# Every third weight block's remainder from a negated copy on ScalarE and an adding DMA, in place of a VectorE subtraction

## The chip, the cores and the metric

The kernel runs on one NeuronCore of a Trainium2 chip: TensorE for the products, VectorE and ScalarE for elementwise work, GpSimd, and SyncE (SP), which issues most transfers. The metric is the device time of one execution in microseconds (us); smaller is better. In the profile TensorE is PE (its weight loads are PEld), VectorE is DVE, ScalarE is ACT, GpSimd is POOL, and a q behind an engine's name is its queue.

## The reference

Two layers over 256 tokens of width 2048, all in float32: attention with a residual, then a feed-forward with a residual, and at the end a last norm. Every dense product takes a weight matrix from HBM that is used once.

```python
def rms_norm(x, g):
    y = x * lax.rsqrt(jnp.mean(x * x, axis=-1, keepdims=True) + EPS)
    return y * g

def sq_relu_mlp(h, w1, w2):          # w1 2048 x 8192, w2 8192 x 2048
    return jnp.square(jax.nn.relu(h @ w1)) @ w2

def reference(x, ...):
    for i in range(2):
        hn = rms_norm(x, mixer_norms[i])
        if i == 0:
            x = x + neighbourhood_attention(hn, na_wqkv, na_rpb, na_wo)
        else:
            x = x + dilated_attention(hn, dil_wqkv, dil_wo)
        g, w1, w2 = ffns[i]
        x = x + sq_relu_mlp(rms_norm(x, g), w1, w2)
    return rms_norm(x, final_norm)
```

The first attention has 16 heads with a learned bias over a 64-wide grid; the second has three groups of 8 heads with different dilations, and a softmax over all three together.

## The kernel before

**Weight blocks.** All weights are cut into 400 blocks of 4 x 128 rows and 512 columns (1 MB). One block is one step of the program. In order: 48 blocks for q, k and v of the first attention (four groups of 8 for q and k and 4 for v), 16 for its output, 128 for the first feed-forward (four times 16 of w1 and 16 of w2), 72 and 8 for the second attention, 128 for the second feed-forward.

**Precision by two parts.** TensorE's fast float32 form (F32R) keeps fewer bits, so each operand is cut into a rounded part (`hi`; for weights the tile wh) and the remainder (`lo`; tile wl), and the product of the two remainders is dropped. `split` (line 103) makes both: ScalarE copies the source into the rounded form (line 104), VectorE subtracts that from the source (line 105). `prep(i, u)` (line 86) does so for half u of block i, a tile of 128 x 1024; a block's first half is the first two of its four 128-row pieces.

**Two forms of product.** `gemm_cols` (lines 134 and 136): the weights stand still and the activations stream, two products for each piece and column tile. These are the q and k blocks and w1, in column groups of four blocks k = 0 to 3. Block k = 0 takes its quarters as two column tiles with the first half, the same with the second half, then the other two column tiles, so the second half is wanted after one quarter; the others go piece by piece. `gemm_rows` (lines 155 to 157): the activations stand still, three products; these are v, the output projections and w2, piece by piece.

**Order.** The order on each engine is the order in which the loop at the end of `tile_encoder` issues the work (line 736 on). In step i, after the second quarter, the first half of block i + 2 is prepared (line 746), after the step its second half (line 759), then the load of block i + 5 is issued on SP (line 760). Work that belongs to a step goes between: `evac` copies finished sums out of PSUM (the copies at line 144 on ScalarE, the additions at 146 and 271 on VectorE), `post` and the tasks do norms, softmax (Exp at line 407), the square of the feed-forward (line 474) and the cutting of the activations hT, on the same two engines.

**Buffers.** `wpool` holds three whole blocks, so the load of block i + 5 goes where block i + 2 lay and waits until both its halves have been read. `hlpool` holds four halves of wh and four of wl, that is two blocks: the half of block i + 2 goes where that half of block i lay, and its preparation waits until TensorE has read that for the last time.

Of the kernel before, what the change touches and what calls it, by code (L numbers as in the profile page):

```python
# [8 lines left out]
F32 = mybir.dt.float32  # L9
F32R = mybir.dt.float32r  # L10
AF = mybir.ActivationFunctionType
ALU = mybir.AluOpType
AX = mybir.AxisListType

P = 128
# [11 lines left out]


class Step:
    """One weight block [4 x 128, 512], the products that it takes part in (in four  # L30
    quarters) and the work that goes with them: tasks have a part on the tensor engine
    after a quarter, evac reads the finished sums, post follows."""

    def __init__(self, src, quarters):
        self.src = src
# [7 lines left out]
def tile_encoder(ctx: ExitStack, tc: tile.TileContext, ins, out):  # L43
    nc = tc.nc
# [13 lines left out]
    x = const.tile([P, 2, D], F32, name="x")  # L58
# [9 lines left out]

    x_in = ins["x"].rearrange("(t p) d -> p t d", p=P)

# [1 line left out]
    steps = []  # L72

    def load(i):
# [11 lines left out]
    def prep(i, u):  # L86
        if i >= len(steps):
            return
        s = steps[i]
        hi = hlpool.tile([P, 2, 512], F32R, name="wh", tag="wh")  # L90
        lo = hlpool.tile([P, 2, 512], F32R, name="wl", tag="wl")
        part = s.w[:, 2 * u:2 * u + 2, :]
        if i:
            split(hi, lo, part)
        else:
            for a in range(2):
                split(hi[:, a], lo[:, a], part[:, a])
        s.hi[u], s.lo[u] = hi, lo
# [6 lines left out]
        nc.vector.tensor_tensor(out=dst_lo, in0=src, in1=dst_hi.bitcast(F32), op=ALU.subtract)  # L105

    def three(o, left, right, start, stop):
        """o += left.T @ right, both in two parts; the product of the two rests is below float32."""
        nc.tensor.matmul(o, left[0], right[0], start=start, stop=False)  # L109
        nc.tensor.matmul(o, left[0], right[1], start=False, stop=False)  # L110
        nc.tensor.matmul(o, left[1], right[0], start=False, stop=stop)  # L111

# [1 line left out]
    def gemm_cols(w, col, xT, nk, done):  # L114
        acc = {}
        made = []
# [39 lines left out]
        nc.tensor.matmul(o, xh, wl, start=False, stop=False)  # L156
        nc.tensor.matmul(o, xl, wh, start=False, stop=stop)  # L157

# [1 line left out]
    def gemm_rows(w, col, xT, ks, acc, first_k, last_k, apart=False):  # L160
        made = []
        for k in ks:
# [10 lines left out]
            made.append(s)  # L173
        return made

# [1 line left out]
    class Norm:  # L177
        def __init__(self, n, perm):
            self.n, self.perm = n, perm
# [68 lines left out]
            nc.vector.tensor_copy(self.r, self.r_ps[:, 0, 0:4].rearrange("p (t u) -> p t u", u=2)[:, :, 0])  # L248

    def rsqrt_mean(ss):  # L250
        """1 / sqrt(mean + eps) of the sums of squares: a root, its reciprocal and one step of Newton's on it."""
        a = small.tile([P, 2], F32, name="ms", tag="ms", bufs=2)
        nc.vector.tensor_reduce(out=a, in_=ss, op=ALU.add, axis=AX.X)
        nc.vector.tensor_scalar(out=a, in0=a, scalar1=1.0 / D, scalar2=EPS, op0=ALU.mult, op1=ALU.add)
        r = small.tile([P, 2], F32, name="rstd", tag="rstd", bufs=2)
        nc.scalar.sqrt(r, a)
        nc.vector.reciprocal(r, r)
        u = small.tile([P, 2], F32, name="ru", tag="ru", bufs=2)
        nc.vector.tensor_tensor(out=u, in0=r, in1=r, op=ALU.mult)
        nc.vector.tensor_tensor(out=u, in0=u, in1=a, op=ALU.mult)  # L260
        nc.vector.tensor_scalar(out=u, in0=u, scalar1=-0.5, scalar2=1.5, op0=ALU.mult, op1=ALU.add)
        nc.vector.tensor_tensor(out=r, in0=r, in1=u, op=ALU.mult)
        return r

    # x += rows; at the end of a sublayer the next norm is begun
    def add_rows(made, col_block, acc, norm, chunk_done):
        cs = slice(col_block * 512, (col_block + 1) * 512)
        if norm is not None and norm() in fin and col_block == NB - 1:
# [19 lines left out]
        later.append((i, pe, post, quarter))  # L288

    def pending_norm(get):  # L290
        """Hooks behind the steps that finish x's column blocks."""
        def chunk_done(step, c):
            i = steps.index(step)
            for half in range(2):
                at(i + 1, lambda half=half: get().transposes(c, half), lambda half=half: get().parts(c, half),
                   quarter=1 + half)
            if c == NB - 1:
                at(i, None, lambda: get().rstd())
                at(i + 2, lambda: get().rows(), lambda: get().rows_out())
                if get().perm:  # L300
                    at(i + 3, lambda: get().cols(), lambda: get().cols_out())
        return chunk_done

# [1 line left out]
    norms = [Norm(0, False), None, None, None]  # L305

    n0 = norms[0]
# [11 lines left out]
        return hi, lo  # L319

    class NaHeads:
        """Four heads: their q, k, v, bias and the steps from scores to outputs."""

        def __init__(self, c):
            self.c = c

        # bias[c + 64 e, h, o, 63 - c'] is for the query (2 t + e, c) and the key (o - 2 + 2 t, c')
        def load_bias(self, h):
            if h == 0:
                self.bias = big.tile([P, 4, 6, GRID_W], F32, name="bias", tag="big")  # L330
# [68 lines left out]
            split(t[:, h, 0, :], t[:, h, 1, :], self.o[:, 0, :])  # L399

    def softmax(p):
        """p [P, 2, n]: each row of n becomes its softmax."""
        m = small.tile([P, 2], F32, name="m", tag="m")
        nc.vector.tensor_reduce(out=m, in_=p, op=ALU.max, axis=AX.X, negate=True)
        z = small.tile([P, 2], F32, name="sum", tag="sum")
        for tb in range(2):
            nc.scalar.activation(p[:, tb, :], p[:, tb, :], AF.Exp, bias=m[:, tb:tb + 1],
                                 accum_out=z[:, tb:tb + 1])
        nc.vector.reciprocal(z, z)
        for tb in range(2):  # L410
            nc.vector.tensor_scalar(out=p[:, tb, :], in0=p[:, tb, :], scalar1=z[:, tb:tb + 1], scalar2=None,
                                    op0=ALU.mult)
# [4 lines left out]
    for c in range(4):  # L417
# [5 lines left out]
        i = steps.index(made[0])  # L423
# [5 lines left out]
        i = steps.index(made[0])  # L429
# [3 lines left out]
               lambda H=H, h=h, task=task: getattr(H, task + "_post")(h))  # L433

    def rows_apart(pair, xT, acc, finish):
        """The last two blocks of a sum of four: the first half of the tokens through both, then the second."""
        for tb, s in enumerate(pair):
            def quarter(s, n, tb=tb):
                for a in (n % 2 * 2, n % 2 * 2 + 1):
                    products(acc[tb], pair[n // 2], xT[2 + n // 2], a, slice(tb * P, (tb + 1) * P),  # L440
                             False, n == 3 and a == 3)
            s.quarters = quarter
            s.evac.append(lambda tb=tb: finish(tb, acc))
# [16 lines left out]
    out_rows(ins["na_wo"], na_oT, 4, lambda: norms[1], begin_norm(1, False),  # L460
             [(c, k) for c in range(3) for k in range(3)] + [(c, 3) for c in range(3)] + [(3, k) for k in range(4)])

# [1 line left out]
    def ffn(norm, w1, w2, next_norm, next_done):  # L464
        for g in range(4):
            hT = [None] * 4
# [14 lines left out]

    ffn(norms[1], ins["ffn0_w1"], ins["ffn0_w2"], lambda: norms[2], begin_norm(2, True))

# [1 line left out]
    n2 = norms[2]  # L485
    dil_oT = [None] * 2
    rope = {}
# [142 lines left out]
    out_rows(ins["dil_wo"], dil_oT, 2, lambda: norms[3], begin_norm(3, False),  # L630
             [(0, 0), (1, 0), (0, 1), (1, 1), (2, 0), (2, 1), (3, 0), (3, 1)])

# [1 line left out]
    class Final:  # L634
        perm = False

# [30 lines left out]
        def finish(self, tb, acc):  # L667
            cs = slice((NB - 1) * 512, D)
            nc.vector.tensor_tensor(out=x[:, tb, cs], in0=x[:, tb, cs], in1=acc[tb], op=ALU.add)
            self.square(NB - 1, tb)  # L670
            ms = small.tile([P, 1], F32, name="fms", tag="fms", bufs=2)
            nc.vector.tensor_scalar(out=ms, in0=self.ss[:, tb, NB - 1:], scalar1=1.0 / D,
                                    scalar2=self.part[:, tb:tb + 1], op0=ALU.mult, op1=ALU.add)
            # -2 / sqrt(ms): a root, its reciprocal and one step of Newton's on it; the gain has the factor -1/2
            r = small.tile([P, 1], F32, name="fr", tag="fr", bufs=2)
            nc.scalar.sqrt(r, ms)
            nc.vector.reciprocal(r, r)
            u = small.tile([P, 1], F32, name="fu", tag="fu", bufs=2)
            nc.vector.scalar_tensor_tensor(out=u, in0=r, scalar=ms, in1=r, op0=ALU.mult, op1=ALU.mult)
            nc.vector.scalar_tensor_tensor(out=r, in0=u, scalar=-3.0, in1=r, op0=ALU.add, op1=ALU.mult)  # L680
            for c in range(NB):
                cs = slice(c * 512, (c + 1) * 512)
                if c == 0:
                    nc.vector.tensor_scalar(out=x[:, tb, cs], in0=x[:, tb, cs], scalar1=r, scalar2=None,
                                            op0=ALU.mult)
                elif c == NB - 1:
                    nc.vector.scalar_tensor_tensor(out=x[:, tb, cs], in0=x[:, tb, cs], scalar=r, in1=self.g[:, cs],
                                                   op0=ALU.mult, op1=ALU.mult)
                else:
                    nc.scalar.activation(x[:, tb, cs], x[:, tb, cs], AF.Copy, scale=r)  # L690
                nc.sync.dma_start(self.o_v[:, tb, cs], x[:, tb, cs])
# [3 lines left out]
    at(len(steps) + 104, None, fin[0].halve)  # L695
    ffn(norms[3], ins["ffn1_w1"], ins["ffn1_w2"], lambda: fin[0], None)

# [1 line left out]
    for i, pe, post, q in later:  # L699
        if pe is None:  # L700
            steps[i].post.append(post)
# [129 lines left out]
```

## Time and profile before

| what | us |
|---|---|
| median of two runs | 2322.54 (2321.96 to 2323.12) |
| span of the profiled execution | 2320.3 |
| busy, TensorE products | 2300.7 |
| busy, VectorE | 1406.0 |
| busy, ScalarE | 1092.6 |
| busy, GpSimd | 0.7 |
| median time from issue to landing of a weight block | 4.8 |

The profiled execution's own span is 2.2 us under the median of the runs. The busy times overlap, so they do not add up to the span; a busy share near 100% says that the engine is the one that the others follow, and idle time on the others costs nothing by itself. TensorE's granted clock was 0.999 over the whole span.

In the lines of groups, "L105 DVE TENSOR_TENSOR wl<-w,wh ... x802 | 972.8, 1221 | ..." reads: line 105, VectorE, 802 instructions, 972.8 us in all, 1221 ns each; behind the second bar stands how long the engine had been idle ahead of them and what ended that. In the timeline a line begins with its start and its length in us; x2 merges two instructions in a row. A DMA line ends with KB per transfer and the median us from issue to landing.

### The profile page before, as it was taken

What the parts mean: (1) busy time and instruction counts of PE and PEld (TensorE: products, weight loads), DVE (VectorE), ACT (ScalarE), POOL (GpSimd) and SP (SyncE); (2) the same over time, 40 slices, a digit from 0 to 9 for tenths busy, and PEclk for the clock granted to TensorE, in tenths of its full rate; (3) what the DMA queues carried; (4) which work ended last, traced back from release to release, by engine and by line L of the source; (5) the groups of instructions that cost most, each with busy time, mean ns of one, the idle gap of its engine ahead of it and who ended that gap; (6) DMA issues with size and microseconds to landing.
All of it is one profiled execution on the core that took longest, in us unless ns stands there. A gap on an engine that the chain in (4) does not pass through costs nothing.

```text
span 2320.3 us, 29178 instructions
## 1 busy us (share of the span) xinstructions
PE 2300.7 (99%) x11956; PEld 1963.1 (85%) x11956; DVE 1406.0 (61%) x1635; ACT 1092.6 (47%) x1390; POOL 0.7 (0%) x6
## 2 busy tenths in 40 slices
PE   8999999999999999999999999999999999999998
PEld 7888888888888888888888888888888888888886
DVE  6666765654555555566777667756654654555654
ACT  6444545543443453455444544445543543543443
POOL 0000000000000000000000000000000000000000
PEclk9999999999999999999999999999999999999999
DMA  7555655555555555555555545454555555555553
GB/s 248 169 175 176 191 182 170 182 197 200 182 187 194 185 196 189 193 181 188 189 179 184 177 164 181 164 181 169 191 192 193 182 200 187 189 187 200 200 192 135
DMA packets 73862, 430.36 MB, mean 185 GB/s; under 512 B 19776, under 2 KB 20352, under 8 KB 22528
## 3 DMA queue, kind: packets, MB, share of 16 engines
q1 hardware_dynamic: 73056, 426.80, 54.3%
q8 instruction: 93, 1.52, 0.3%
q10 hardware_dynamic: 672, 1.70, 0.2%
q14 instruction: 41, 0.34, 0.0%
HBM read 426.38 MB, written 2.10 MB: 185 GB/s over the span
## 4 chain that ended last, share of the span: by engine, by line
PE 98%; DMA 1%; DVE 1%; ACT 0%; issue 0%; SPq 0%; ACTq 0%; DVEq 0%
PE acc L134 33%; PE acc L136 17%; PE acc L156 15%; PE acc L155 15%; PE acc L157 15%; PE misc L194 1%; DMA bias<-in_rpb_dram 0%; PE misc L111 0%; PE misc L110 0%; PE misc L109 0%; DVE wl L105 0%; PE misc L593 0%; PE misc L553 0%; PE misc L380 0%; ACT wh L104 0%
## 5 line engine op out<-in xcount | busy, mean ns | idle before, releaser
L105 DVE TENSOR_TENSOR wl<-w,wh 128x1024 fp32r<-128x1024 f32 (+1 forms) x802 | 972.8, 1221 | 735.8 <-ACT wh L104 733.6
L104 ACT CAST wh<-w 128x1024 fp32r<-128x1024 f32 (+1 forms) x802 | 834.9, 1049 | 936.9 <-PE acc L157 460.2
L134 PE MATMUL acc<-xT,wh 128*128 128x512 f32 x3328 | 1178.5, 399 | 0.9 <-ACT wh L104 0.9
L136 PE MATMUL acc<-xT,wl 128*128 128x256 f32 x3328 | 935.0, 281 | 2.3 <-DVE wl L105 2.3
L134 PEld LDWEIGHTS acc<-xT,wh 128*128 128x128 f32 x3328 | 626.4, 188 | 150.4 <-ACT wh L104 1.9
L136 PEld LDWEIGHTS acc<-xT,wl 128*128 128x128 f32 x3328 | 629.8, 189 | 3.7 <-DVE wl L105 3.2
L155 PE MATMUL acc<-wh,hT 128*128 128x512 f32 x1024 | 399.5, 390 | 0.0
L156 PE MATMUL acc<-wl,hT 128*128 128x512 f32 x1024 | 399.0, 390 | 0.0
L157 PE MATMUL acc<-wh,hT 128*128 128x512 f32 x1024 | 398.9, 390 | 0.0
L157 PEld LDWEIGHTS acc<-wh,hT 128*128 128x128 f32 x1024 | 192.3, 188 | 39.9
L155 PEld LDWEIGHTS acc<-wh,hT 128*128 128x128 f32 x1024 | 192.3, 188 | 39.7
L156 PEld LDWEIGHTS acc<-wl,hT 128*128 128x128 f32 x1024 | 192.3, 188 | 39.4
L155 PE MATMUL acc<-wh,xT 128*128 128x512 f32 x320 | 126.7, 396 | 0.0
L156 PE MATMUL acc<-wl,xT 128*128 128x512 f32 x320 | 125.2, 391 | 1.1 <-DVE wl L105 1.1
L157 PE MATMUL acc<-wh,xT 128*128 128x512 f32 x320 | 124.9, 390 | 0.0
L144 ACT COPY b<-acc 128x512 f32<-128x512 f32 x104 | 60.7, 586 | 64.8 <-PE acc L136 59.1
L146 DVE TENSOR_TENSOR z<-acc,b 128x512 f32<-128x512 f32 x104 | 71.5, 691 | 25.8 <-ACT b L144 25.2
L155 PE MATMUL acc<-wh,oT 128*128 128x512 f32 x192 | 76.6, 399 | 0.0
L157 PE MATMUL acc<-wh,oT 128*128 128x512 f32 x192 | 75.0, 391 | 0.0
L156 PE MATMUL acc<-wl,oT 128*128 128x512 f32 x192 | 74.9, 390 | 0.0
L156 PEld LDWEIGHTS acc<-wl,xT 128*128 128x128 f32 x320 | 60.2, 188 | 13.1 <-DVE wl L105 1.8
L157 PEld LDWEIGHTS acc<-wh,xT 128*128 128x128 f32 x320 | 60.1, 188 | 12.5
(123 smaller groups left out, 1044.9 us busy)
## 6 DMA issues: line engine op xcount, KB each, us to landing
w<-in_ffn_w_dram SPq DMA_DIRECT2D x256, 1024.0 KB, 4.8
w<-in_dil_wqkv_dram SPq DMA_DIRECT2D x72, 1024.0 KB, 4.8
w<-in_na_wqkv_dram SPq DMA_DIRECT2D x47, 1024.0 KB, 4.9
w<-in_na_wo_dram SPq DMA_DIRECT2D x16, 1024.0 KB, 4.9
w<-in_dil_wo_dram SPq DMA_DIRECT2D x8, 1024.0 KB, 4.8
bias<-in_rpb_dram SPq DMA_DIRECT2D x32, 96.0 KB, 8.7
out_dram<-x SPq DMA_DIRECT2D x8, 256.0 KB, 2.5
x<-in_x_dram SPq DMA_DIRECT2D x3, 512.0 KB, 7.8
```

Of the source, the lines that this page charges most:

```text
L104: nc.scalar.copy(dst_hi, src)
L105: nc.vector.tensor_tensor(out=dst_lo, in0=src, in1=dst_hi.bitcast(F32), op=ALU.subtract)
L134: nc.tensor.matmul(o, s.hi[a // 2][:, a % 2, cs], xt.rearrange("p h t -> p (h t)"), start=first, stop=False)
L136: nc.tensor.matmul(o[:, :T], s.lo[a // 2][:, a % 2, cs], xt[:, 0, :], start=False, stop=last)
L144: nc.scalar.copy(b, acc[j][:, :, T:])
L146: nc.vector.tensor_tensor(out=z, in0=acc[j][:, :, :T], in1=b, op=ALU.add)
L155: nc.tensor.matmul(o, xh, wh, start=start, stop=False)
L156: nc.tensor.matmul(o, xh, wl, start=False, stop=False)
L157: nc.tensor.matmul(o, xl, wh, start=False, stop=stop)
L194: nc.tensor.transpose(self.tp[:, a, tb * P:(tb + 1) * P], x[:, tb, kt * P:(kt + 1) * P], ident)
```

## The change

In `prep`, a block whose number is over 4 and a multiple of three no longer goes through `split`. ScalarE makes the rounded copy as before, then writes the negated rounded part into wl, and GpSimd issues a transfer inside SBUF that adds the source w to wl. wl ends as w - wh, as before. VectorE has no part in these blocks. That holds for 132 of the 400 blocks, 264 halves. All other edits in the file take out comments and docstrings; the change adds five lines, so line 104 becomes 109, 105 becomes 110, 474 becomes 479, and so on.

```diff
     def prep(i, u):
...
         part = s.w[:, 2 * u:2 * u + 2, :]
-        if i:
+        if i > 4 and i % 3 == 0:
+
+            nc.scalar.copy(hi, part)
+            nc.scalar.mul(lo, hi.bitcast(F32), -1.0)
+            nc.gpsimd.dma_start(lo.bitcast(F32), part, accum_op=ALU.add)
+        elif i:
             split(hi, lo, part)
```

On ScalarE, in a w1 group of the first feed-forward, a column group's sums are copied out (b), squared (z) and cut (hT), and behind that stand the casts of the weight halves. Before:

```order
L144 COPY b<-acc 128x512 x2
L104 CAST wh<-w 128x1024
L474 ACTIVATE z<-z 128x512 x2
L104 CAST hT<-z 128x2x256 x2
L104 CAST wh<-w 128x1024 x7
L144 COPY b<-acc 128x512 x2
```

And now, in the group whose third block is one of the 132:

```order
L149 COPY b<-acc 128x512 x2
L109 CAST wh<-w 128x1024
L479 ACTIVATE z<-z 128x512 x2
L109 CAST hT<-z 128x2x256 x2
L95 CAST wh<-w 128x1024
L96 ACTIVATE wl<-wh 128x1024
L95 CAST wh<-w 128x1024
L96 ACTIVATE wl<-wh 128x1024
L109 CAST wh<-w 128x1024 x4
```

The first two casts behind hT are each followed by a negated copy now, so the second of them and all behind it stand one or two instructions later.

On SP's queue, in the first feed-forward, the loads of weight blocks follow each other, each with the semaphores it waits for (DMAHW for transfers of the hardware queues, DMASW for transfers issued by GpSimd). Before:

```order
L81 DMA w<-in_ffn_w_dram 128x2048 [waits DMAHW7_49,DVE_49]
L81 DMA w<-in_ffn_w_dram 128x2048 [waits DMAHW0_49,DVE_49]
L81 DMA w<-in_ffn_w_dram 128x2048 [waits DMAHW1_49,DVE_49]
L81 DMA w<-in_ffn_w_dram 128x2048 [waits DMAHW2_49,DVE_49]
L81 DMA w<-in_ffn_w_dram 128x2048 [waits DMAHW3_49,DVE_49]
```

And now:

```order
L81 DMA w<-in_ffn_w_dram 128x2048 [waits DMASW3_49,DMAHW7_49,DMASW2_49,Activation_49]
L81 DMA w<-in_ffn_w_dram 128x2048 [waits DMAHW0_49,DVE_49]
L81 DMA w<-in_ffn_w_dram 128x2048 [waits DMAHW1_49,DVE_49]
L81 DMA w<-in_ffn_w_dram 128x2048 [waits DMASW5_49,DMAHW2_49,DMASW4_49,Activation_49]
L81 DMA w<-in_ffn_w_dram 128x2048 [waits DMAHW3_49,DVE_49]
```

Every third load waits for two adding transfers of GpSimd's queue in place of VectorE.

## The prediction

> **What bounds the kernel now.** I read the page's busy table and its chain of waits first, then the costliest groups, the DMA view, and at last the timeline at the places where a weight block is cut up. The page:
>
> ```profile
> span 2320.3 us, 29178 instructions
> ## 1 busy us (share of the span) xinstructions
> PE 2300.7 (99%) x11956; PEld 1963.1 (85%) x11956; DVE 1406.0 (61%) x1635; ACT 1092.6 (47%) x1390; POOL 0.7 (0%) x6
> ...
> PE 98%; DMA 1%; DVE 1%; ACT 0%; issue 0%; SPq 0%; ACTq 0%; DVEq 0%
> ```
>
> TensorE is busy for 2300.7 of 2320.3 us and carries 98% of the chain that ended last. All idle time that any change around it can win is 2320.3 - 2300.7 = 19.6 us, 0.8%. A change that leaves the products alone can therefore not be faster by the 2% that a measurement of this kernel tells from no change (46 us); it can only be hidden or cost something. What matters is how early each weight half is ready. The groups and the DMA view:
>
> ```profile
> L105 DVE TENSOR_TENSOR wl<-w,wh 128x1024 fp32r<-128x1024 f32 (+1 forms) x802 | 972.8, 1221 | 735.8 <-ACT wh L104 733.6
> L104 ACT CAST wh<-w 128x1024 fp32r<-128x1024 f32 (+1 forms) x802 | 834.9, 1049 | 936.9 <-PE acc L157 460.2
> ...
> L136 PE MATMUL acc<-xT,wl 128*128 128x256 f32 x3328 | 935.0, 281 | 2.3 <-DVE wl L105 2.3
> ```
>
> ```profile
> q1 hardware_dynamic: 73056, 426.80, 54.3%
> ...
> w<-in_ffn_w_dram SPq DMA_DIRECT2D x256, 1024.0 KB, 4.8
> ...
> bias<-in_rpb_dram SPq DMA_DIRECT2D x32, 96.0 KB, 8.7
> ...
> dmask<-in_dmask_dram ACTq DMA_DIRECT2D x1, 512.0 KB, 3.4
> ```
>
> A cast of a half takes 1.05 us and waits for PE to free the buffer; the subtraction takes 1.22 us and waits for the cast. The products that use wl wait 2.3 us in all 3328 cases together. So the preparation is early now, but it is tied to PE: it starts when PE frees one of the four buffer pairs, and has to be done when PE comes round to it. That stretch is the **lead**; read it at one half of a feed-forward w2 block (cast, subtraction, first product with wl):
>
> ```profile
> 1060.84 1.05 ACT L104 CAST wh<-w 128x1024 fp32r<-128x1024 f32 x1 [1.65 <-PE acc L157]
> ...
> 1061.92 1.22 DVE L105 TENSOR_TENSOR wl<-w,wh 128x1024 fp32r<-128x1024 f32 x1 [0.59 <-ACT wh L104]
> ...
> 1063.52 1.05 ACT L104 CAST wh<-w 128x1024 fp32r<-128x1024 f32 x1 [1.62 <-PE acc L157]
> ...
> 1066.23 1.05 ACT L104 CAST wh<-w 128x1024 fp32r<-128x1024 f32 x1 [1.67 <-PE acc L157]
> ...
> 1068.98 0.39 PE L156 MATMUL acc<-wl,hT 128*128 128x512 f32 x1
> ```
>
> The cast of a half of block 183 starts at 1060.84, its wl is ready at 1063.14, PE wants it at 1068.98: the lead is 8.14 us, of which cast and subtraction use 2.3. Casts follow each other by 2.7 us (1063.52 to 1066.23), a half step, so the lead is three half steps.
>
> **The change part by part.** The blocks are counted 0 to 399 in program order; those over 4 that three divides are 132, so 264 halves.
>
> *Taken from VectorE:* 264 x 1.22 = 322 us. It lies beside PE, which waits 2.3 us for it at L136; worth nothing, bounded by the 19.6 us above. *Added to ScalarE:* 264 negated copies of the size of the cast, 264 x 1.05 = 277 us, which makes it 59% busy; behind each wait, in its queue, the next casts, the copies of finished sums (L144), Square and Exp. They come about 1 us later and have leads of the same kind; I give that nothing of its own. *Added on GpSimd's queue:* 264 adding transfers, each behind the negated copy of its half. GpSimd has 0.7 us of work, so nothing else queues there.
>
> So wl of such a half is ready after cast, negated copy, two hand-overs and the transfer. Two casts in a row take 1.99 us (rows below), a hand-over 0.03 (1060.84 + 1.05 = 1061.89 to 1061.92); with DMA hand-overs I take 2.15 us. With D the time from issue to landing, PE stalls by 2.15 + D - lead wherever that is above zero, and per block by the worse of its halves, since a stall for the first half gives the second one as much.
>
> *D is the open price.* No row of before shows an adding transfer, or one inside SBUF, or a queue of GpSimd. From below: 512 KB loaded by ScalarE's queue landed after 3.4 us, 1024 KB after 4.8: 1.4 us for each further 512 KB, 2.0 fixed. If the transfer reads two streams and writes while it reads, it is like the 1024 KB load: 4.8. If source, old value and result pass one after the other, it is 2.0 + 3 x 1.4 = 6.2. From above: the slowest kind of transfer, bias in small pieces, 8.7. A gain below 3.4 is excluded, as the same 512 KB must at least be written. I take 6.2, between the ends and near their middle: an engine that reads what it adds to, and a queue without any issue cost of its own in these rows, are both more than the plain load shows.
>
> The Trainium skill, "DMA: Bandwidth & Descriptors", section on the anatomy of one DMA on the gpsimd path, has 2.0 us fixed plus bytes over 436 GB/s, and "Collectives: The Full Stack", section on the bandwidth ceiling, says that an adding transfer runs at half rate because it reads two sources, not because of the addition. By both an estimate of D is 2.0 + 1.05 MB / 436 GB/s = 4.4 us, and the sum below would be 26 us; no run here shows either yet.
>
> *Where the lead is shorter.* Third block of a w1 group (block 174): its casts queue behind Square and the splitting of hT. Second half of the first block of a column group (348): PE wants it after one quarter, not two. First block of a q group behind v (36): behind the softmax.
>
> ```profile
> 1012.91 1.99 ACT L104 CAST wh<-w 128x1024 fp32r<-128x1024 f32 x2
> ...
> 1018.65 0.28 PE L136 MATMUL acc<-xT,wl 128*128 128x256 f32 x1
> ...
> 2015.56 1.05 ACT L104 CAST wh<-w 128x1024 fp32r<-128x1024 f32 x1 [1.77 <-PE acc L134]
> 2018.39 1.05 ACT L104 CAST wh<-w 128x1024 fp32r<-128x1024 f32 x1 [1.77 <-PE acc L134]
> ...
> 2025.61 0.28 PE L136 MATMUL acc<-xT,wl 128*128 128x256 f32 x1
> ...
> 236.00 1.98 ACT L104 CAST wh<-w 128x1024 fp32r<-128x1024 f32 x2
> ...
> 238.35 0.39 PE L136 MATMUL acc<-xT,wl 128*128 128x256 f32 x1 [0.77 <-DVE wl L105]
> ```
>
> Leads of 5.74, 7.22 and 2.35 us; the last has no room today (PE waits 0.77). With 2.15 + 6.2 = 8.35 us needed:
> - 43 w2 blocks, lead 8.14: 43 x 0.21 = 9.0
> - 11 third blocks of w1 groups: 11 x 2.61 = 28.7
> - 14 first blocks of column groups (10 in w1, 4 in the dilated layer): 14 x 1.13 = 15.8
> - 3 first q blocks behind v: 3 x 6.0 = 18.0
> - 21 other w1 blocks, leads like three half steps of 2.83 us (2015.56 to 2018.39), so 8.5: 2 in all
> - the other 40, in attention and output projections, as the mean of the first three kinds, 53.5 / 68 = 0.79: 31
>
> Sum 104.5 us on the span of 2320.3; the median of the runs shown (2322.54) is 2.2 above the span: **2427 us**.
>
> *The moved wait of the loads.* SP's queue waits for the last reader of a weight buffer (the queue's own waits, and its issues in the view of w, with ns least, median and most):
>
> ```profile
> SPq L81 <- DVE wl L105: 2055.7, 392, 14.8
> ...
> L81 SPq DMA_DIRECT2D w<-in_ffn_w_dram x256: 327/328/328, 387.2 to 2286.5; - x128
> ```
>
> That reader is now, in every third load, the landed transfer; buffers go round by three, so it is always the same one. The load is due five half steps (13.6 us) after the second half's cast, and is there after 2.15 + D + 4.8 us plus 0.33 for its issue: room 6.3 - D, 0.1 us at D = 6.2. Above it casts are late too, with other ScalarE work queued behind them; but each stall of PE lengthens the three steps by as much, so I add nothing. The load behind it on SP starts hardly later than now.
>
> **The rivals.**
>
> *Hidden but for the short leads.* The transfer is as quick as a 1024 KB load, D = 4.8, 6.95 us needed. Then only the 11 third blocks (11 x 1.21 = 13.3), the 3 q blocks (3 x 4.6 = 13.8) and the mixed 40 (8) stall: 35 us, 2358 us, within 2%. For it: 54.3% of 16 engines leaves room, and the load of this buffer itself waits, so the second half's transfer runs alone. Against: no price for the issue and the read-back. By the Trainium skill's two rules above it would be 2349, this rival again. It turns to slower by 2% at D about 5.2.
>
> *The DMA engines become the bound.* 426.8 MB are 407 loads of 1024 KB, 0.543 x 2320.3 / 407 = 3.1 us of all engines each. What is free, 0.457 x 2320.3 = 1060 us, is 4.0 us for each adding transfer. If one costs as two loads, 6.2, the excess is 264 x 2.2 = 581 us: 2900 us. Against it: two streams of 512 KB are one load, 3.1. The upper end D = 8.7 alone, with 10.85 us needed, gives 116 + 56 + 51 + 26 + 54 (21 w1 blocks x 2.55) + 131 = 434 us: 2757 us.
>
> *Other side: VectorE was what PE waited for.* In the attention layers the subtraction queues behind softmax work (the 0.77 us above). Taking a third of it away could free PE there. All idle time of PE is 19.6 us, so at best 2303 us, and only if D is below 2.35 - 2.15 = 0.2 us at those places, which the 3.4 us row excludes for blocks that the change touches.
>
> **How the numbers follow.** Forecast, D from 5.2 to 8.7: 0.60. Hidden, D below 5.2: 0.25. DMA-bound, or D above 8.7: 0.13. Gain: 0.02. Slower by over 2% is 0.60 + 0.13 = 0.73, within 2% 0.25, faster 0.02. The range goes from D = 4.2 (6.35 us needed: 6.7 + 12 + 4 = 23 us, 2345) to the upper end, 2750; below it about 0.05 is left, above 0.14. The forecast's own range is 2370 to 2750.
>
> **What would show it.** The adding transfers in the DMA view with a median of 5.2 to 8.7 us to landing; PE idle before L136 and L156 with the DMA of wl as releaser, about 100 us in all, most of it at third blocks of w1 groups and first blocks; VectorE's L105 group down to 538 calls, ScalarE near 59%; SP waiting for the wl transfer. A median below 5 us would make the forecast wrong downwards; a q1 and GpSimd queue near 100% together, or weight loads landing well after 4.8 us, upwards; a PE that waits for wh rather than wl would say that the held load, not D, sets the price.

## The result, and the profile after

| | before | after |
|---|---|---|
| median of the runs, us | 2322.54 | 2443.87 (2443.22 to 2444.52) |
| span of the profiled execution, us | 2320.3 | 2442.6 |
| TensorE busy, us | 2300.7 | 2339.0 |
| TensorE idle (span less busy), us | 19.6 | 103.6 |
| granted TensorE clock over the span | 0.999 | 0.986 |

The change makes the kernel slower: ratio 1.0524 (95% interval 1.0493 to 1.0554), against 2427 us forecast. The total of the prediction is nearly right. Its parts are not, and the experiments are mostly about them.

The page of the kernel after: its span, busy times and instruction counts by engine, the chain of work that ended last, and the two queues that carry nearly all transfers (packets, MB, share of the time of 16 DMA engines):

```profile
span 2442.6 us, 30254 instructions
...
PE 2339.0 (96%) x11956; PEld 1978.7 (81%) x11956; DVE 1091.6 (45%) x1371; ACT 1366.0 (56%) x1654; POOL 227.9 (9%) x270
...
q1 hardware_dynamic: 73056, 426.80, 48.7%
q0 software_dynamic: 38016, 138.43, 29.6%
...
PE 58%; DMA 24%; issue 15%; ACT 1%; POOL 1%; DVE 0%; SPq 0%; POOLq 0%; ACTq 0%; DVEq 0%
```

The chain was 98% PE and 1% DMA before; now 24% of it is DMA. Of the 122.3 us that the span grew, 84.0 are more idle time of TensorE (103.6 - 19.6) and 38.3 are a longer busy time for the same 11956 products (2339.0 - 2300.7). So there are two things to explain, a wait and slower products.

The transfers in the view of issues (KB each, median us from issue to landing), then the waits of whole instructions (us in total, times, longest):

```profile
w<-in_ffn_w_dram SPq DMA_DIRECT2D x256, 1024.0 KB, 5.0
wl<-w POOLq DMA_DIRECT2D x264, 512.0 KB, 4.9
...
w<-in_na_wqkv_dram SPq DMA_DIRECT2D x47, 1024.0 KB, 5.8
...
bias<-in_rpb_dram SPq DMA_DIRECT2D x32, 96.0 KB, 11.2
```

```profile
PE acc L141 <- DMA wl<-w: 41.1, 31, 5.9
PE acc L161 <- DMA wl<-w: 37.9, 17, 4.4
```

TensorE waits 79.0 us for the adding transfers, in 48 places out of 264. That is nearly all of the 84.0 us. The median to landing is only 4.9 us where 6.2 was taken. Where then do the waits come from? The same figure by stretch, first the first attention with its output (40 to 420 us), then the first feed-forward (400 to 1090 us):

```profile
DMA to landing us min/median/max: 4.6/6.4/11.7
```

```profile
DMA to landing us min/median/max: 4.5/4.7/6.2
```

The transfer has a quiet price, some 4.7 us, and a busy one, up to 11.7 us in attention.

To place the loss, each of the 400 blocks was given a step on TensorE, from its first product to the first product of the next block, and the steps of the two traces were subtracted. The sums in us:

| where | excess of after |
|---|---|
| first attention and its output (blocks 0 to 63) | 66.9 |
| first feed-forward | 13.9 |
| second attention | 25.2 |
| second feed-forward | 16.2 |

Fifty-five per cent of the loss is in the 64 blocks of the first attention, 16% of them in number. Within these, two places carry it. The blocks of q and k come in groups of 12 with v; blocks 6 and 9 of each group carry 29.8 us, and the last block of a group with the first of the next (11, 12, 23, 24, 35, 36, 47, 48) carry 34.2 us. All experiments below give these two sums again, under the names **blocks 6/9** and **group ends**.

**A quiet place.** In the timeline of after, the second half of block 75, the fourth block of a w1 column group (cast, negated copy, issue), and the chain of waits at the same place:

```profile
531.97 1.05 ACT L95 CAST wh<-w 128x1024 fp32r<-128x1024 f32 x1 [0.68 <-PE acc L139]
533.05 1.06 ACT L96 ACTIVATE wl<-wh 128x1024 fp32r<-128x1024 f32 x1
534.41 0.86 POOL L97 DMA_DIRECT2D wl<-w  x1 [1.96 <-ACT wl L96]
```

```profile
534.41 4.55 DMA wl<-w
```

Cast to issue is 534.41 - 531.97 = 2.44 us. The hand-over from the end of ScalarE's copy (534.11) to GpSimd's start is 0.30 us, not the few hundredths that ScalarE and VectorE had between them. With 4.55 us of transfer wl is usable 7.0 us after the cast starts. The prediction had 8.35.

**A busy place.** Block 9 of the first group in after: GpSimd's two issues, and SP's loads and bias pieces around them.

```profile
58.03 0.86 POOL L97 DMA_DIRECT2D wl<-w  x1 [12.64 <-PE acc L141]
61.40 0.86 POOL L97 DMA_DIRECT2D wl<-w  x1 [2.51 <-ACT wl L96]
```

```profile
57.42 3.89 SPq L337 DMA_DIRECT2D bias<-in_rpb_dram  x2
71.57 0.33 SPq L81 DMA_DIRECT2D w<-in_na_wqkv_dram  x1
71.95 2.57 SPq L337 DMA_DIRECT2D bias<-in_rpb_dram  x2
```

The chain of waits shows what TensorE got, and the timeline how long it stood:

```profile
58.03 10.05 DMA wl<-w
```

```profile
68.12 0.80 PE L161 MATMUL acc<-wl,xT 128*128 128x512 f32 x1 [3.97 <-DMA wl<-w]
```

The same kind of transfer that takes 4.55 us in the quiet place takes 10.05 us here. It shares the DMA engines with a weight load issued at 56.36, with the bias pieces issued at 57.42, which are many small packets, and from 61.40 on with the transfer of the second half. On SP the next load (71.57) waits until these adding transfers have landed, and the bias pieces stand behind that load in the same queue: they are issued at 71.95. Before, the two pieces of that place went out at 60.37:

```profile
60.37 3.41 SPq L332 DMA_DIRECT2D bias<-in_rpb_dram  x2
```

What that does to VectorE shows in the addition of the mask to the bias, after and then before:

```profile
82.59 1.76 DVE L343 TENSOR_TENSOR bias<-bias,namask 128x1536 f32<-128x1536 f32 x1 [15.29 <-DMA bias<-in_rpb_dram]
```

```profile
72.79 1.76 DVE L338 TENSOR_TENSOR bias<-bias,namask 128x1536 f32<-128x1536 f32 x1 [7.61 <-DMA w<-in_na_wqkv_dram]
```

(The profile names a weight load as what ended the wait before; the addition reads no weights, so nothing rests on that name here.) VectorE stands 15.29 us in place of 7.61, and the softmax behind it, with it the preparation of block 12, comes 9.8 us later than before.

**The slower products.** The stretches of 2 us around that stall in after (window, length, busy time of PE, PEld, DVE, ACT and POOL with instruction counts, granted clock, DMA share, GB/s):

```profile
64.00:66.00 2.00, 0.15 (x1) 0.00 (x0) 1.06 (x1) 1.85 (x2) 0.00 (x0) 1.00 1.02 296
66.00:68.00 2.00, 0.00 (x0) 0.00 (x0) 1.30 (x2) 0.00 (x0) 0.00 (x0) 0.68 1.03 307
68.00:70.00 2.00, 1.88 (x5) 1.49 (x6) 0.00 (x0) 0.00 (x0) 0.00 (x0) 0.50 1.11 261
70.00:72.00 2.00, 2.00 (x6) 1.61 (x5) 0.00 (x0) 0.00 (x0) 0.00 (x0) 0.50 0.58 125
72.00:74.00 2.00, 2.00 (x10) 1.71 (x10) 0.00 (x0) 0.78 (x1) 0.00 (x0) 0.61 0.76 164
74.00:76.00 2.00, 2.00 (x11) 1.66 (x10) 0.00 (x0) 1.55 (x2) 0.00 (x0) 1.00 0.96 373
```

The last product ahead of the stall ends at 64.15 (0.15 us busy in the first row). The mean clock of 0.68 in the second row puts the fall to 0.50 at about 66.7, some 2.6 us later and still inside the stall. The 0.61 of the fifth row puts the way back at about 73.6, some 5.4 us after the first product behind the stall (68.12). Five or six products fit in 2 us in place of ten or eleven. The stall of 3.97 us so costs some 3 us again (5.4 us at half clock). The Trainium skill, "TensorE: Matmul & The Clock Gate", section on the HAM clock gate, has TensorE at half clock after about 3.4 us of idling and at full clock again after about as long under load. The rows above differ from both figures: the fall comes sooner and the way back later. At the next long wait (4.50 us, ending at 97.77) it is the other way round: the clock falls 4.2 us after the last product and is back 3.1 us after the next one.

Over the span the granted clock says the same: (1 - 0.986) x 2442.6 = 34 us, against 2 before. Not all of that falls on products. Up to the last product the clock stands at half in thirteen stretches of 3.4 or 6.8 us, nine of them in the first attention and its output and four in the second attention. TensorE is busy for 53.0 us of these, so some 26 of the 38.3 us of longer products are the clock. The other 12 us were not traced.

### The profile page after: what moved, and what is told of

Read it like the earlier page. It is cut to its first block, busy times and chain, and to the rows that moved or that the text cites. A ratio compares the mean times of both kernels' runs of the same rounds, so it can differ in the third digit from the quotient of the medians.

```text
span 2442.6 us, 30254 instructions
## 1 busy us (share of the span) xinstructions
PE 2339.0 (96%) x11956; PEld 1978.7 (81%) x11956; DVE 1091.6 (45%) x1371; ACT 1366.0 (56%) x1654; POOL 227.9 (9%) x270
## 4 chain that ended last, share of the span: by engine, by line
PE 58%; DMA 24%; issue 15%; ACT 1%; POOL 1%; DVE 0%; SPq 0%; POOLq 0%; ACTq 0%; DVEq 0%
DMA wl<-w 15%; PE acc L139 14%; PE acc L161 12%; PE acc L162 12%; PE acc L160 12%; PE acc L141 7%; DMA w<-in_ffn_w_dram 5%; DMA w<-in_na_wqkv_dram 2%; POOL wl L97 1%; DMA x<-in_x_dram 0%; DMA w<-in_dil_wqkv_dram 0%; ACT wh L109 0%; DMA bias<-in_rpb_dram 0%; PE misc L199 0%; PE misc L598 0%
## 5 line engine op out<-in xcount | busy, mean ns | idle before, releaser
L110 DVE TENSOR_TENSOR wl<-w,wh 128x1024 fp32r<-128x1024 f32 (+1 forms) x538 | 653.5, 1220 | 986.1 <-ACT wh L109 984.4
L109 ACT CAST wh<-w 128x1024 fp32r<-128x1024 f32 (+1 forms) x538 | 560.3, 1046 | 615.5 <-PE acc L162 313.1
L141 PEld LDWEIGHTS acc<-xT,wl 128*128 128x128 f32 x3328 | 632.0, 190 | 54.7 <-DMA wl<-w 53.5
L97 POOL DMA_DIRECT2D wl<-w x264 | 227.3, 861 | 2194.1 <-ACT wl L96 1787.6
L95 ACT CAST wh<-w 128x1024 fp32r<-128x1024 f32 x264 | 277.3, 1051 | 221.9 <-PE acc L139 112.5
L96 ACT ACTIVATE wl<-wh 128x1024 fp32r<-128x1024 f32 x264 | 280.0, 1061 | 8.4
L161 PE MATMUL acc<-wl,xT 128*128 128x512 f32 x320 | 132.7, 415 | 33.6 <-DMA wl<-w 25.4
L160 PE MATMUL acc<-wh,xT 128*128 128x512 f32 x320 | 131.3, 410 | 0.0
L162 PE MATMUL acc<-wh,xT 128*128 128x512 f32 x320 | 130.4, 408 | 0.0
L151 DVE TENSOR_TENSOR z<-acc,b 128x512 f32<-128x512 f32 x104 | 71.4, 691 | 67.2 <-ACT b L149 66.7
```

What stands on the lines that cost most here:

```text
L95: nc.scalar.copy(hi, part)
L96: nc.scalar.mul(lo, hi.bitcast(F32), -1.0)
L97: nc.gpsimd.dma_start(lo.bitcast(F32), part, accum_op=ALU.add)
L109: nc.scalar.copy(dst_hi, src)
L141: nc.tensor.matmul(o[:, :T], s.lo[a // 2][:, a % 2, cs], xt[:, 0, :], start=False, stop=last)
L151: nc.vector.tensor_tensor(out=z, in0=acc[j][:, :, :T], in1=b, op=ALU.add)
```

## The experiments

Each is compared with the kernel before, run on the same chip (2323 us). The edits are to the kernel after unless another is named. Each median is of four executions, for the third experiment of ten and for the tenth of eleven. Block sums come from the one profiled execution of each.

### Which blocks pay

**One: only the 85 blocks of the two feed-forwards are changed.**

```diff
-        if i > 4 and i % 3 == 0:
+        if i % 3 == 0 and (64 <= i < 192 or i >= 272):
```

> The 85 blocks of the two feed-forwards alone are made with the adding transfer; the 47 in the attention layers and output projections go back to VectorE. Theory A (each block pays for itself: the copies and hand-overs take 2.43 us from the cast, the transfer 4.6 us when alone, and PE waits for what the lead lacks): the step differences between the two traces over these blocks sum to about 31 us, so 2353 us, within 2% of before, and TensorE's mean granted clock back at 0.998 or more. Rival B (the price is spread evenly, by 277 us more work on ScalarE and fuller DMA engines): 85/132 of 121 us, 78 us, so 2400 us.

Measured 2352.27 us (2347.28 to 2355.77), ratio 1.0124 (1.0109 to 1.0139), granted clock 0.998.

**Two: only the other 47 blocks are changed.**

```diff
-        if i > 4 and i % 3 == 0:
+        if i > 4 and i % 3 == 0 and not (64 <= i < 192 or i >= 272):
```

> The reverse: only the 47 blocks in the attention layers and output projections are made with the adding transfer. Theory A: the step differences sum to about 88 us, so 2410 us, with a granted clock near 0.986 as in the change. Rival B (spread evenly): 47/132 of 121 us, 43 us, so 2366 us. If the two parts sum to 121 us they do not act on each other.

Measured 2411.95 us, ratio 1.0382 (1.0367 to 1.0398), clock 0.986. The two excesses, 29.1 and 88.8 us, add up to 117.9 of the 121 us. So 85 of 132 blocks cost a quarter of the loss and 47 cost three quarters, and the clock falls almost only with the latter. The split by steps of TensorE is confirmed by taking the parts alone.

**Three: the change only where the lead is long.** In each feed-forward the second and fourth blocks of w1 column groups, and the w2 blocks of the first three quarters but one; 51 blocks. All others are made as before.

```diff
-        if i > 4 and i % 3 == 0:
+        f = i - (64 if i < 192 else 272)
+        if i % 3 == 0 and 0 <= f < 128 and i not in (114, 354) and (i % 2 if f % 32 < 16 else f < 112):
```

> The adding transfer only at 51 feed-forward blocks whose lead in the trace of before is over 7.8 us: second and fourth blocks of w1 groups, and w2 blocks but those next to a norm. Theory A (7.0 us from the cast to the landed transfer, so a longer lead hides it whole): no difference, 2323 to 2330 us, clock 0.998 or more. Rival B (each transfer costs something by its load on the DMA engines and ScalarE): 51/132 of the 121 us of the change, 47 us, 2370 us.

Measured 2326.72 us, ratio 1.0015 (1.0006 to 1.0025). The page of this kernel:

```profile
PE 2302.3 (99%) x11956; PEld 1961.4 (84%) x11956; DVE 1281.7 (55%) x1533; ACT 1198.9 (52%) x1492; POOL 88.6 (4%) x108
```

VectorE has 124 us less to do than before (1406.0 - 1281.7), ScalarE 106 more, and the time is 3 to 4 us longer: two late w2 blocks in the second feed-forward, by 1.24 and 1.98 us, are nearly all that remains. Where the lead covers 7.0 us the change costs nothing, and it wins nothing either.

### What of the price is the transfer, the addition, ScalarE

**Four: VectorE adds, in place of the transfer.** ScalarE's negated copy stays.

```diff
-            nc.gpsimd.dma_start(lo.bitcast(F32), part, accum_op=ALU.add)
+            nc.vector.tensor_tensor(out=lo, in0=part, in1=lo.bitcast(F32), op=ALU.add)
```

> ScalarE writes the negated rounded part as in the change, but VectorE adds the source to it, so no adding transfer is left and the weight loads wait for VectorE again. Theory A: the 264 more ScalarE copies lie beside PE but for the short leads; wl is 1 us later than before and 3.6 us earlier than in the change: 2325 to 2340 us. Rival B (ScalarE's queue carries the price): over 2380 us.

Measured 2341.49 us, ratio 1.0080 (1.0065 to 1.0095), just above what was expected. 18.2 us are at the group ends, blocks 6/9 pay nothing, and the rest of the kernel next to nothing. Block 12 in this kernel's timeline:

```profile
85.32 1.03 ACT L95 CAST wh<-w 128x1024 fp32r<-128x1024 f32 x1
...
86.40 0.50 PE L139 MATMUL acc<-xT,wh 128*128 128x512 f32 x1 [1.26 <-ACT wh L95]
87.47 1.23 DVE L97 TENSOR_TENSOR wl<-w,wl 128x1024 fp32r<-128x1024 f32 x1 [1.21 <-ACT wl L96]
88.75 0.39 PE L141 MATMUL acc<-xT,wl 128*128 128x256 f32 x1 [1.85 <-DVE wl L97]
```

TensorE waits twice, once for wh since the cast of the second half stands behind the softmax and the negated copy of the first on ScalarE, and once for wl. The two waits are only 1.26 and 1.85 us long, and still the granted clock is at half behind them (a stretch of 2 us, in the columns of the stretches above):

```profile
90.00:92.00 2.00, 2.00 (x9) 1.82 (x8) 2.00 (x4) 0.96 (x2) 0.00 (x0) 0.50 0.75 307
```

Up to the last product the clock stands at half for 17.1 us in this kernel, and TensorE is busy for 15.1 us of these, so some 7.5 of the 18.2 us are the clock. ScalarE's 264 copies are thus free everywhere but behind the softmax of a group, where there was no room before.

**Five: the transfer copies and doesn't add.** wl holds w rather than the remainder; the addition is what it leaves out.

```diff
-            nc.gpsimd.dma_start(lo.bitcast(F32), part, accum_op=ALU.add)
+            nc.gpsimd.dma_start(lo.bitcast(F32), part)
```

> The transfer on GpSimd's queue is a plain copy of w over wl, so the addition is left out and wl holds w itself; all else is as in the change. Theory A1 (the second stream that an adding transfer reads is what makes it long): landing 3.4 to 3.9 us in place of 4.9, 16-engine time per transfer about 1.4 us in place of 2.7; the feed-forward stalls nearly go and the attention ones shrink: 2340 to 2380 us. Rival A2 (the software queue's fixed time is what counts, whatever the transfer does): landing above 4.4 us and 2420 us or more.

Measured 2386.3 us, ratio 1.0269 (1.0252 to 1.0286), somewhat above the 2340 to 2380 us of theory A1 and far below the rival's 2420. Its queue and its row in the view of issues:

```profile
q0 software_dynamic: 38016, 138.43, 14.6%
...
wl<-w POOLq DMA_DIRECT2D x264, 512.0 KB, 3.3
```

The second stream costs 4.9 - 3.3 = 1.6 us to landing. Of the 16 engines' time a plain transfer takes 0.146 x 2386.7 / 264 = 1.32 us, an adding one 0.296 x 2442.6 / 264 = 2.74 us, twice as much. The Trainium skill, "Collectives: The Full Stack", section on the bandwidth ceiling, has the adding step of a collective at half rate because it reads two sources; the engine time here, with no collective, agrees (a factor of 2.1). In the feed-forwards the excess falls from 30.1 to 4.6 us, in the second attention from 25.2 to 10.0, but in the first attention and its output only from 66.9 to 51.8. There the price is mostly not the addition. At block 9 of the first group the plain copy even took longer than the adding one (11.27 against 10.05 us), and so did TensorE's wait:

```profile
56.90 11.27 DMA wl<-w
```

```profile
68.21 0.80 PE L161 MATMUL acc<-wl,xT 128*128 128x512 f32 x1 [5.20 <-DMA wl<-w]
```

### What makes the first attention dear

**Six: the bias pieces in long runs.** Runs of 384 values in place of 64, in the same number of bytes and transfers; the bias is then not the reference's.

```diff
-                                  bass.AP(rpb.tensor, (self.c * 4 + h) * RPB + (5 - e) * 31 - 48,
-                                          [[1, GRID_W], [31, 6], [1, GRID_W]]))
+                                  bass.AP(rpb.tensor, (self.c * 4 + h) * 440 + (5 - e) * 31 - 48,
+                                          [[1, GRID_W], [GRID_W, 6], [1, GRID_W]]))
```

> The change with the bias loaded as runs of 384 neighbouring values for each partition in place of six runs of 64, the same bytes in a sixth of the pieces; the bias values are wrong, so this leaves the right bias out. Theory S (the adding transfer of blocks 9, 21, 33 and 45 is long because its packets alternate with thousands of 256-byte pieces): these transfers land in 5 to 7 us in place of 10 to 13, their 27 us of stalls fall to under 8, and the bias comes earlier too: about 2410 us. Rival H (the held load does it): the four stalls stay and the time is 2435 us or more.

Measured 2416.08 us (2409.92 to 2421.65), ratio 1.0403 (1.0384 to 1.0422). Blocks 6/9 fall from 29.8 to 7.7 us; the group ends stay at 29.7. The stall at block 9 of the first group in this kernel:

```profile
66.08 0.50 PE L161 MATMUL acc<-wl,xT 128*128 128x512 f32 x1 [1.56 <-DMA wl<-w]
```

TensorE waits 1.56 us where it waited 3.97, and uses the half issued at 58.39 after 7.7 us, in place of 10.1 us (58.03 to 68.12). Packets under 512 bytes go from 24000 to 11712. So at blocks 6/9 the dear thing is the many small packets of the bias beside the transfer.

**Seven: the bias on ScalarE's queue.** It no longer stands behind the held loads on SP.

```diff
-                nc.sync.dma_start(self.bias[e * GRID_W:(e + 1) * GRID_W, h],
+                nc.scalar.dma_start(self.bias[e * GRID_W:(e + 1) * GRID_W, h],
```

> The change with the bias loads of the first attention issued on ScalarE's queue, not on SP's. Theory H (a weight load that waits on SP for an adding transfer holds back the bias pieces issued behind it, so VectorE gets its bias late): VectorE's wait for bias falls from 61 us to under 25, and the stalls at blocks 11, 12, 23, 24, 35, 36, 47 and 48, 34 us in the change, fall to the 18 us that the version with VectorE's addition shows there: about 2428 us. Rival S (the pieces only share the DMA engines with the transfer, whoever issues them): those stalls and those at blocks 9, 21, 33 and 45 (27 us) stay, 2440 us or more, and up to 20 us more, since 32 issues of 0.6 us now stand in ScalarE's queue.

Measured 2400.29 us (2397.93 to 2403.73), ratio 1.0337 (1.0321 to 1.0352). Its bias in the waits and in the view of issues:

```profile
DVE bias L343 <- DMA bias<-in_rpb_dram: 17.2, 4, 5.3
...
bias<-in_rpb_dram ACTq DMA_DIRECT2D x32, 96.0 KB, 7.4
```

The kernel after has this wait in the same view as:

```profile
DVE bias L343 <- DMA bias<-in_rpb_dram: 61.4, 4, 16.0
```

The wait of VectorE goes from 61.4 to 17.2 us. The group ends go from 34.2 to -5.2 us, where 18 were expected, and the time is below the 2428 us expected; blocks 6/9 stay at 28.3. At this point the reading was that the held bias is the whole price of the group ends.

**Eight: blocks 6/9 of the first attention left as before.**

```diff
-        if i > 4 and i % 3 == 0:
+        if i > 4 and i % 3 == 0 and not (i < 48 and i % 12 in (6, 9)):
```

> The change without the eight blocks whose transfers meet the bias loads (6, 9, 18, 21, 30, 33, 42, 45), which go back to VectorE. Theory A with S: the step differences at these blocks (30 us) go, and of those at blocks 11 and 12 and their like (34 us) the part above the 18 us that ScalarE's copies alone cost: 2444 - 30 - 16 = 2398 us. Rival (the long stalls come from ScalarE and VectorE in this layer, not from the transfers): 2425 us or more.

Measured 2403.22 us, ratio 1.0347 (1.0332 to 1.0362). Blocks 6/9 are at 0, and the group ends fall as well, from 34.2 to 22.6 us. The bias of the first group in this kernel, and the first product of block 12 that waits:

```profile
74.68 1.76 DVE L343 TENSOR_TENSOR bias<-bias,namask 128x1536 f32<-128x1536 f32 x1 [7.58 <-DMA w<-in_na_wqkv_dram]
...
89.61 0.58 PE L141 MATMUL acc<-xT,wl 128*128 128x256 f32 x1 [4.27 <-DMA wl<-w]
```

VectorE's wait is back at what it was before (7.61), and TensorE still waits 4.27 us. So 11.6 us of the group ends came from blocks 6/9, through SP; 22.6 remain though the bias is in time.

**Nine: both, seven and eight in one kernel.**

> The change without the eight blocks whose transfers meet the bias loads, and with the bias loads on ScalarE's queue. If the two mechanisms (sharing with the bias pieces, 30 us; bias held back on SP, 34 us) are separate and together the whole price of the first attention but for some 3 us, what stays is the feed-forwards (31 us and 3 at the end) and the dilated layer (26 us), less some 5 us that the earlier bias saves: 2375 to 2382 us. If one of them is only another face of the other, it is no faster than the better of the two alone, 2400 us.

Measured 2404.4 us (2397.96 to 2412.59), ratio 1.0343 (1.0327 to 1.0359): missed, it is no faster than either alone. Blocks 6/9 are at 0, the group ends at 24.1. Block 12 in this kernel:

```profile
80.82 1.01 POOL L97 DMA_DIRECT2D wl<-w  x1 [79.52 <-ACT wl L96]
84.58 0.86 POOL L97 DMA_DIRECT2D wl<-w  x1 [2.75 <-ACT wl L96]
```

```profile
87.52 0.58 PE L141 MATMUL acc<-xT,wl 128*128 128x256 f32 x1 [4.68 <-DMA wl<-w]
```

The bias is not what is late here. ScalarE casts the first half of block 12 no later than before, where it is the second of two casts in a row:

```profile
78.37 1.04 ACT L95 CAST wh<-w 128x1024 fp32r<-128x1024 f32 x1
```

```profile
78.11 1.99 ACT L104 CAST wh<-w 128x1024 fp32r<-128x1024 f32 x2
```

The transfer was issued 2.45 us behind its cast, as in the quiet place, and TensorE still waits 4.68 us. So the reading after the seventh run falls. The sums of blocks 0 to 63 say it in one row each:

| kernel | blocks 6/9 | group ends | all of blocks 0 to 63 |
|---|---|---|---|
| after | 29.8 | 34.2 | 66.9 |
| VectorE adds (four) | 0 | 18.2 | 18.1 |
| transfer copies (five) | 21.3 | 29.0 | 51.8 |
| bias in long runs (six) | 7.7 | 29.7 | 40.8 |
| bias on ScalarE's queue (seven) | 28.3 | -5.2 | 25.2 |
| blocks 6/9 left out (eight) | 0 | 22.6 | 26.1 |
| both (nine) | 0 | 24.1 | 27.6 |

About 25 us stay in the seventh, eighth and ninth, and VectorE's version, which has no transfer at all, already pays 18.1 of them. So the two prices are not separate: cutting either one takes away some 41 us (66.9 - 26), and cutting both takes away no more. The likely reading is this. With the bias on ScalarE's queue the stall at block 9 comes first, and TensorE's delay gives the softmax and block 12 the time that they lack: the same wait is paid once, at block 9. Without that stall it is paid at block 12. The kernel after pays both at once: a stall at blocks 6/9 that also holds the loads and the bias on SP, so that the softmax is later by more than the stall and gains nothing by it. The sums fit this reading; no run tests it by itself.

**Ten: the bias on ScalarE's queue in the kernel before.**

```diff
-                nc.sync.dma_start(self.bias[e * GRID_W:(e + 1) * GRID_W, h],
+                nc.scalar.dma_start(self.bias[e * GRID_W:(e + 1) * GRID_W, h],
```

> The kernel before, with only the bias loads moved from SP's queue to ScalarE's. Theory H (before too had its bias late because the pieces stood behind waiting weight loads on SP): VectorE's wait for bias falls from 23 us, and the idle time of TensorE at blocks 11 and 12 and their like goes: 5 to 9 us faster than before, at most the 19.6 us that TensorE is idle there, so 2314 to 2318 us. Rival (the 32 issues in ScalarE's queue of 0.6 us each delay casts as much as the early bias saves): 2320 to 2328 us.

Measured 2323.14 us, ratio 0.9996 (0.9987 to 1.0005): no gain. VectorE waits for the bias there as long as before (22.6 us in four waits, 23.4 before), and those waits cost TensorE next to nothing. No version was found that beats the kernel before.

### What was not tried

A fourth weight buffer, which might take the hold off SP, was not tried. The second attention's 25.2 us were read in the trace and tested only by the fifth run. Seven blocks carry 24.5 us of them (195, 207, 219, 222, 243, 255 and 258), and the transfers of their first halves took 7.5 to 9.9 us. At block 207 GpSimd's and SP's issues of the kernel after stand together, and the chain gives the length of the second half's transfer:

```profile
1286.09 0.86 POOL L97 DMA_DIRECT2D wl<-w  x1 [14.69 <-ACT wl L96]
1286.16 0.33 SPq L81 DMA_DIRECT2D w<-in_dil_wqkv_dram  x1
1289.62 0.86 POOL L97 DMA_DIRECT2D wl<-w  x1 [2.67 <-ACT wl L96]
```

```profile
1289.62 7.89 DMA wl<-w
```

It took 7.89 us beside the weight load and the first half's transfer, against 4.55 in the quiet place. Over the kernel after, the 112 transfers with no weight load and no bias piece beside them took 4.5 to 6.1 us, 4.6 at the median, though nearly all of them run beside that of the other half. The 7 with no bias piece but a weight load beside them for over 5 us took 7.9 to 9.9 us. A longer transfer also meets more, so this is no proof: shared DMA engines are the likely cause, but no run took the load away. The clock's 26 us are read from the granted clock and were not isolated either. Four issues on GpSimd came 0.96 or 2.25 us after the end of the copy ahead of them, in place of 0.29; no row explains them.

## Why the prediction was right in sum and wrong in parts

- **TensorE as the bound, VectorE's relief worth nothing.** Right. The third run takes 124 us from VectorE and the time grows by 0.15%.
- **2.15 us to issue.** Measured 2.44; the hand-over to GpSimd is 0.30 us and the 0.16 for all hand-overs was too little.
- **D, the open price, 6.2 us.** Over-sized. It is 4.6 us at the median where no weight load and no bias piece runs beside it, and 4.9 over all. The choice rested on the thought that source, old value and result pass one after the other (three times 1.4 us). The plain copy against the adding one fits two streams better: 1.6 us more to landing and twice the engine time. The row that was nearest is the one of the rival of a hidden transfer, the 1024 KB load of 4.8 us; the estimate of 4.4 us from the Trainium skill's two pages was nearer than 6.2 as well.
- **Terms of the feed-forwards.** The leads were read rightly. With the measured 7.0 us in place of 8.35 the 11 third blocks give 11 x (7.0 - 5.74) = 13.9 us; their steps grew by 13.1 (predicted 28.7). The first blocks of column groups, lead 7.22, should then be free and took 6.0 in w1, 4.8 of it in the first feed-forward, where the transfers of their second halves took 5.3 to 5.7 us; the w2 blocks, lead 8.14, took 8.5, of which 3.1 are at the last blocks of the program. In all 30.1 us where the terms have 9.0 + 28.7 + 11.3 + 2 = 51.0.
- **Three first q blocks behind v, 18.0 us.** Near in size: blocks 12, 24 and 36 carry 16.5 us in the kernel after and 17.6 in the ninth run. The way there was another, so that the size is in part luck. TensorE waits for the first half (6.7 us from issue to use in the ninth run, 80.82 to 87.52), where the prediction took the second half as the worse one, and some 6 of the 16.5 us are the clock.
- **ScalarE's copies, "nothing of its own".** Right outside the first attention, wrong in it: 18.2 us remain when VectorE adds, some 7.5 of them by the clock.
- **The other 40, 31 us, as the mean of the rest, and the four first blocks of the second attention.** This is the step that failed. With the q blocks these are 31 + 18.0 + 4.5 = 53.5 us; the two attentions with their outputs took 92.1. The mean of quiet places was put on places where the transfer shares the engines with the bias (10.05 us) or runs beside a weight load (7.89 us). The four first blocks of the second attention took 0.5 us in place of 4.5; seven others there took the 24.5. So the sign that most of the idle time would stand at third and first blocks of the feed-forwards did not come: these have 19.1 us of the loss.
- **"The load behind it on SP starts hardly later than now."** False there. The room of 6.3 - D was worked out right, 1.4 us at the median D of 4.9, but D is up to 11.7 in attention, so the load goes late, and the bias pieces behind it on SP go with it: 71.95 in place of 60.37 us. VectorE's wait rose from 15.8 + 7.6 to 61.4 us.
- **The clock.** It stands nowhere in the sum. Stalls were priced at their own length; many of them are followed by slow products, some 26 us in all.
- **The upper end, 2757 us.** The term of the 21 other w1 blocks is 10.85 - 8.5 = 2.35 us each, not 2.55, so the sum gives 2752; nothing else hangs on it.

So two errors had opposite signs: 21 us too much in the feed-forwards from a D too large, 39 us too little in attention from sharing, the held queue and the clock. That the total came within 17 us is luck. The prediction had said that a median landing below 5 us would make the forecast wrong downwards. The median is 4.9, and the time is 17 us above the forecast: a median over 264 transfers, most of them with room to spare, doesn't speak for the 48 that TensorE waits for. Of the rival with the DMA engines as the bound, nothing came as a whole: q0 and q1 together have 78%, but in single stretches of the first attention the share is at 1.

## What to carry to other kernels

A preparation that moves to a transfer is priced against the lead of each place where it is used, and with the length that it has beside the other transfers of that place, not with one median. What stands behind a held transfer on the same queue must be followed to its last user; here a load that waited for the adding transfer kept back the bias of the next softmax. And where TensorE is the bound, a stall also slows the products behind it: here one of about 4 us cost 1.5 to 3 us more by the clock, and two waits of 1.26 and 1.85 us were enough for it to fall.

## What was not expected of the hardware

- An adding transfer inside SBUF of 512 KB lands after 4.5 to 6.1 us (4.6 at the median) when no weight load and no bias piece runs beside it. Over the whole kernel the median is 4.9 us, that of a plain one 3.3 us (lowest 2.8); the adding one takes twice the DMA engines' time (2.74 against 1.32 us). Beside a weight load and bias pieces in packets under 512 bytes it took 10.05 us, a plain one 11.27; with the bias in longer runs the adding one took at most 7.7 us at the same place.
- The granted clock fell to 0.50 some 2.6 us after the last product, stood there for 6.8 us, and came back 5.4 us after products had begun again. In the fourth run two waits of 1.26 and 1.85 us, with products between them, were followed by half clock too.
- GpSimd starts 0.30 us after the ScalarE instruction it waits for, and is busy 0.86 us with each issue.
